# One ScalarE column write ahead of the load of the second x tile

## The chip, the cores and the metric

The kernel runs on one core of one Trainium2 chip. The metric is the device time of one execution in microseconds, as the median of several runs. A profile of one further execution gives the start and duration of every instruction, the DMA packets, and what each engine waited for.

A core has five engines that run side by side, each with its own instruction stream: TensorE (PE in the profile, its weight loads PEld), VectorE (DVE), ScalarE (ACT), GpSimd (POOL) and SyncE (SP). Transfers are issued from the streams of SP, ACT and POOL; a transfer's issue stands in the order of that stream. They are carried by 16 DMA engines that all queues share.

## The reference

One layer of a streaming encoder on an input x of 512 positions by 1024 channels, in float32:

```
xn = RMSNorm(x)
[gate_a | gate_b | gMLP u, v | ssm z | ssm x, B, C | ssm dt] = xn @ W_in
y_a = gMLP spatial gating of u, v
y_b = Mamba-2 mixer (causal conv, chunked scan, SiLU gate, grouped RMSNorm)
m   = sigmoid(gate_a) * (y_a @ P_a) + sigmoid(gate_b) * (y_b @ P_b)
h   = x + m @ W_o
h   = h + ConvGLU-FFN(RMSNorm(h))
out = RMSNorm(h)
```

All that the change touches is how the first product of `xn @ W_in` gets its operands: the transposed input x and the first block of W_in.

## The kernel before

Channels lie on the 128 partitions and the 512 positions along the free dimension. x comes transposed, as eight tiles `xT[0]` to `xT[7]` of 128 channels by 512 positions, 256 KB each. `xT[0]` is part of a slightly larger tile `x0m`, which also carries the weights of the first norm as eight extra columns.

Every float32 operand of a product is split in two halves, `hi` (a rounded copy, made by ScalarE) and `lo` (the rest, made by VectorE). A product takes three matmuls: hi by hi, hi by lo, lo by hi (lines 101, 102 and 104 in `cols`). A block of weights reaches SBUF as `raw`; ScalarE makes `hi` from it and VectorE `lo`.

The first product is called B0 (256 output columns in two PSUM tiles). It runs on x times its norm weight without the division by the norm, which is applied later. It is ordered by k (`BYK`): for each x tile k six matmuls, so that it can begin when `xT[0]` and the first quarter of its weights are there. Its weights come as four transfers of 256 KB (tiles `first0` and `first4`, two k to a transfer). In this text f0a is the transfer for k = 0 and 1, f0b that for k = 2 and 3, f4a and f4b those after them.

The transfers of the start go out in this order from three streams (lines 158 to 171):

```
SP:    x0m, f0a, xT2, xT3, f4a, xT5, f4b, xT7, then the weights C0, wdt, constants, ...
ACT:   xT1, f0b
POOL:  xT4, xT6
```

Then ScalarE and VectorE prepare the operands in a fixed order (lines 189 to 202): `xw0` hi and lo, the weights of f0a hi and lo, `xw1`, `xw2`, the weights of f0b, `xw3`, `xw4`, the weights of f4a, and so on.

Ahead of all that stands a short prologue. GpSimd and VectorE fill constants, among them `one`, a column of ones. PE runs ten warm-up matmuls on a tile of ones (`WARM`, line 143; 20 in the profile, since each takes two passes), whose result nobody reads. ScalarE squares the column `one` in place (line 145); that makes it load its function table at the very start.

The order of this whole first stage is written out by hand for all five streams (`tc.manual_schedule`). After it only PE's order stays written out. The order of the other four streams is set by a planner that walks through a simulated time line of the whole program with its own costs for every instruction and transfer. The planner also allots buffers and places the semaphore waits, in the first stage too: an instruction that overwrites what another wrote waits for it.

Behind B0 come C0 (the same on the next weights), the sums of squares for the norm (`xss`), a small product `dtp`, the broadcast of the norm (`rbp`), and then some 30 products on the normed x, the scan, the gMLP, the merge and the FFN. At the very end one half of the last output tile is written by ScalarE (line 741) and its transfer out is issued from ScalarE's own stream (line 744).

Of the kernel before, what the change touches and what calls it, by code (L numbers as in the profile page):

```python
# [10 lines left out]
AF = mybir.ActivationFunctionType  # L11
# [22 lines left out]
def kernel(  # L34
# [6 lines left out]
    dve, act, pe, pool, sync = nc.vector, nc.scalar, nc.tensor, nc.gpsimd, nc.sync  # L41
# [8 lines left out]
    def T(name, dt=F32):  # L50
        return tp.tile([P, S], dt, tag="t", name=name)
# [4 lines left out]
    def PA(name):  # L56
        return pp.tile([P, S], F32, tag="aux", name=name, bufs=4)
# [4 lines left out]
    def f(t):  # L62
        return t.bitcast(F32)
# [72 lines left out]
    with tc.manual_schedule(engines={E.PE, E.Activation, E.DVE, E.SP, E.Pool}):  # L136
        ones = const.tile([P, P], F32, name="ones")
        pool.memset(ones, 1.0)  # L138
        one = const.tile([P, 1], F32, name="one")
        dve.memset(one, 1.0)  # L140
        warm = PA("warm")
        for i in range(WARM):
            pe.matmul(warm[:, 0:P], lhsT=ones, rhs=ones, start=True, stop=True)  # L143

        act.activation(out=one, in_=one, func=AF.Square)
        ident = const.tile([P, P], F32, name="ident")
        make_identity(nc, ident)
        mhalf = const.tile([P, 16], F32, name="mhalf")
        pool.memset(mhalf, -0.5)
        tri = const.tile([P, P], F32, name="tri")  # L150
        pool.memset(tri, 1.0)
        pool.affine_select(out=tri, in_=tri, pattern=[[1, P]], compare_op=ALU.is_ge, fill=0.0,
                           base=0, channel_multiplier=-1)


        x0 = const.tile([P, S + KD], F32, name="x0m")
        raws = []
        for k in range(KD):
            if k % 4 == 0:
                raw = wp.tile([P, 4, 2 * P], F32, tag="wraw", name=f"first{k}", bufs=4)  # L160
                raws.append(raw)
            if k == 0:
                sync.dma_start(out=x0, in_=x0_in)
                t = x0[:, 0:S]
            else:
                t = T(f"xT{k}")
                {1: act, 4: pool, 6: pool}.get(k, sync).dma_start(out=t, in_=xt_in[:, k, :])
            xT.append(t)
            if k % 2 == 0:
                q = slice(k % 4, k % 4 + 2)  # L170
                (act if k == 2 else sync).dma_start(out=raw[:, q, :], in_=w_in[U_B, k // 4][:, q, :])

        wdt = const.tile([P, KD, HEADS], F32, name="wdt")
        pcol = const.tile([P, R_ALL], F32, name="pcol")
        dtb = const.tile([P, HEADS], F32, name="dtb")
        alog = const.tile([P, HEADS], F32, name="alog")
        ahead_w = []
        for src, name in ((w_in[U_C, 0], "C0w0"), (w_in[U_C, 1], "C0w1")):
            raw = wp.tile([P, 4, 2 * P], F32, tag="wraw", name=name + "r", bufs=4)
            sync.dma_start(out=raw, in_=src)  # L180
            ahead_w.append(raw)
            if name == "C0w0":
                sync.dma_start(out=wdt, in_=wdt_in)
        sync.dma_start(out=pcol, in_=cols_in)
        sync.dma_start(out=dtb, in_=dtb_in[0].partition_broadcast(P))
        sync.dma_start(out=alog, in_=alog_in[0].partition_broadcast(P))


        for k in range(KD):
            h = T(f"xw{k}h", F32R)  # L190
            m = x0[:, S + k:S + k + 1]
            act.activation(out=h, in_=xT[k], func=AF.Copy, scale=m)
            l = T(f"xw{k}l", F32R)
            dve.scalar_tensor_tensor(out=l, in0=xT[k], scalar=m, in1=f(h), op0=ALU.mult, op1=ALU.subtract)
            xw.append((h, l))
            if k % 4 == 0:
                ahead.append([wp.tile([P, 4, 2 * P], F32R, tag=f"w{n}", name=f"B0w{k}{n}") for n in ("hi", "lo")])
            if k % 2 == 0:
                hi, lo = ahead[-1]
                raw, q = raws[k // 4], slice(k % 4, k % 4 + 2)  # L200
                act.activation(out=hi[:, q], in_=raw[:, q], func=AF.Copy)
                dve.tensor_tensor(out=lo[:, q], in0=raw[:, q], in1=f(hi)[:, q], op=ALU.subtract)
# [396 lines left out]
    for i in range(0, 16, 2):  # L599
        ssm_step()  # L600
        ps = cols(w_in, U_Z + i // 2, xn, f"z{i}")
        for q in range(2):
            t = i + q
# [14 lines left out]
    for i in range(0, 8, 2):  # L618
        ps = cols(wpa_in, i // 2, ya, f"pa{i}")
        for q in range(2):  # L620
            t = T(f"m{i + q}")
# [28 lines left out]
    for i in range(0, 8, 2):  # L650
        ps = cols(wo_in, i // 2, ms, f"wo{i}")
        for q in range(2):
            k = i + q
# [172 lines left out]
```

## Time and profile before

| | |
|---|---|
| time, median of 3 runs | 1027.45 us (1027.16 to 1027.64) |
| time of the profiled execution | 1028.71 us |
| its span, first to last instruction | 1027.0 us |
| PE busy | 1014.9 us (99% of the span) |
| VectorE busy | 616.5 us |
| ScalarE busy | 450.2 us |
| first matmul of B0 begins | 6.36 us |
| mean DMA rate over the span | 107 GB/s |
| DMA rate in the first fortieth of the span | 273 GB/s |

The profiled execution takes 1.71 us more than its span, for what lies around the first and last instruction. All times below with two decimals are counted from the start of the span. In a timeline row the first number is the start, the second the duration, both in us; a bracket at the end gives how long the engine had been idle and what ended that. A stream's name with a q (ACTq, SPq) marks an issue of a transfer, not its carrying out. In rows of transfers the last number is the time from issue to landing.

### The profile page before, as it was taken

The page shows a single profiled execution, that of the slowest core. Times are in us where ns is not written, and L with a number is a line of the kernel's source. Part 1 is how long each engine was busy: PE and PEld are TensorE (multiplying, and loading weights), DVE is VectorE, ACT ScalarE, POOL GpSimd, SP SyncE. Part 2 cuts the span into 40 slices and gives each one's busy share as a digit, 9 for nine tenths or more (in the row PEclk, how much of TensorE's full clock was granted, in tenths as well). Part 3 has the DMA queues.
Part 4 walks back from the last instruction along what each step waited for, and adds up shares of the span by engine and source line. Part 5 has one row for each costly group of instructions (what it writes and reads, how often), then busy time and mean ns, then how long its engine had stood idle before and what let it go on. Part 6 is the DMA issues. An engine that isn't in the chain of part 4 may idle for free.

```text
span 1027.0 us, 12488 instructions
## 1 busy us (share of the span) xinstructions
PE 1014.9 (99%) x4856; PEld 840.3 (82%) x4856; DVE 616.5 (60%) x1006; ACT 450.2 (44%) x613; POOL 41.9 (4%) x72
## 2 busy tenths in 40 slices
PE   9999899999999999999999999999999999999997
PEld 7888788888888888888888888888888888888885
DVE  7795987878796554354123445477668677742224
ACT  7465675665564333363322223354444444331122
POOL 1000000220000200000000000000000000000000
PEclk9999899999999999999999999999999999999999
DMA  7323445423333233323322332232223233323302
GB/s 273 110 83 111 151 144 165 143 94 121 114 125 113 72 97 110 113 85 100 102 97 88 103 102 86 100 114 92 91 93 96 91 101 103 97 89 103 99 25 83
DMA packets 36157, 109.85 MB, mean 107 GB/s; under 512 B 4657, under 2 KB 4929, under 8 KB 36097
## 3 DMA queue, kind: packets, MB, share of 16 engines
q1 hardware_dynamic: 35056, 106.68, 31.8%
q0 software_dynamic: 608, 1.58, 0.5%
q8 instruction: 38, 0.62, 0.3%
q10 hardware_dynamic: 432, 0.79, 0.2%
q14 instruction: 23, 0.18, 0.1%
HBM read 106.80 MB, written 2.24 MB: 106 GB/s over the span
## 4 chain that ended last, share of the span: by engine, by line
PE 98%; DMA 1%; issue 0%; DVE 0%; ACT 0%; POOLq 0%; POOL 0%; SPq 0%
PE dn L726 11%; PE vp L526 1%; PE vp L528 1%; PE vp L527 1%; PE pb6p L101 1%; PE pb4p L101 1%; PE pb2p L101 1%; PE pb0p L101 1%; PE pb6p L104 1%; PE pb4p L104 1%; PE pb2p L104 1%; PE pb0p L104 1%; PE pb6p L102 1%; PE pb4p L102 1%; PE pb2p L102 1%; PE pb0p L102 1%
## 5 line engine op out<-in xcount | busy, mean ns | idle before, releaser
L397 ACT ACT_TABLE_LOAD x15 | 19.2, 1283 | 3.1 <-DMA s15bc<-acum_d 1.6
L764 POOL TENSOR_TENSOR fsr<-fs,mhalf 128x1 f32<-128x1 f32 x4 | 2.2, 548 | 354.9 <-DVE fs L762 354.9
L657 ACT ACTIVATE hh<-hT,pcol 128x512 fp32r<-128x512 f32 x8 | 5.8, 722 | 15.0 <-DVE hT L655 15.0
L756 ACT ACTIVATE fj<-htok 128x512 f32<-128x512 f32 x8 | 5.1, 632 | 16.6 <-DVE htok L754 16.6
L345 ACT ACT_TABLE_LOAD x8 | 10.3, 1283 | 3.9 <-DVE B2c L343 3.0
L214 POOL TENSOR_TENSOR hrr<-hrv,mhalf 128x4 f32<-128x4 f32 x1 | 1.0, 1042 | 248.0 <-DVE hrv L212 248.0
L631 DVE TENSOR_TENSOR m<-m,sa 128x512 f32<-128x512 f32 x8 | 5.5, 688 | 8.6 <-ACT sa L630 8.6
L754 DVE TENSOR_TENSOR htok<-dn,htok 128x512 f32<-128x512 f32 x8 | 5.5, 692 | 8.0 <-PE dn L726 7.9
L612 DVE TENSOR_TENSOR yq<-yq,zs 128x512 f32<-128x512 f32 x12 | 8.2, 685 | 1.5 <-ACT zs L611 1.4
L562 PEld LDWEIGHTS sp<-wsT,v 128*128 128x128 f32 x64 | 7.8, 191 | 0.3
L659 DVE SCALAR_TENSOR_TENSOR hl<-hT,pcol,hh 128x512 fp32r<-128x512 f32 x8 | 6.0, 747 | 3.2 <-ACT hh L657 3.2
L562 PE MATMUL sp<-wsT,v 128*128 128x128 f32 x64 | 7.8, 275 | 0.0
L538 DVE BATCH_NORM_STATS2 bst<-v 128x6 f32<-128x128 f32 x32 | 7.1, 280 | 0.3
L534 ACT ACTIVATE v<-vp 128x512 f32<-128x512 f32 x8 | 4.8, 594 | 3.6 <-PE vp L528 3.6
L565 DVE SCALAR_TENSOR_TENSOR sv<-sp,pcol,radd 128x512 f32<-128x512 f32 x8 | 6.0, 746 | 0.0
L343 DVE SCALAR_TENSOR_TENSOR B2c<-B2p,pcol,B2c 128x511 f32<-128x511 f32 (+2 forms) x6 | 4.2, 742 | 2.5 <-ACT B2c L341 2.5
L694 ACT COPY htok<-htp 128x512 f32<-128x512 f32 x8 | 4.7, 588 | 2.3 <-PE htp L692 2.3
L143 PE MATMUL warm<-ones 128*128 128x128 f32 x20 | 4.6, 429 | 1.1 <-POOL ones L138 1.1
L568 DVE TENSOR_TENSOR sv<-sv,gu 128x512 f32<-128x512 f32 x8 | 5.5, 688 | 0.3
L645 DVE TENSOR_TENSOR sb<-sb,m 128x512 f32<-128x512 f32 x8 | 5.5, 689 | 0.1
L343 DVE SCALAR_TENSOR_TENSOR x14c<-x14p,pcol,x14c 128x511 f32<-128x511 f32 (+2 forms) x6 | 4.5, 747 | 1.5 <-ACT x14c L341 1.4
L743 DVE SCALAR_TENSOR_TENSOR htok<-htok,fsr,fnw 128x512 f32<-128x512 f32 x7 | 5.0, 745 | 0.7 <-POOL fsr L764 0.7
(4034 smaller groups left out, 3501.2 us busy)
## 6 DMA issues: line engine op xcount, KB each, us to landing
out_dram<-htok SPq DMA_DIRECT2D x7, 256.0 KB, 2.0
xT<-in_xt_dram SPq DMA_DIRECT2D x4, 256.0 KB, 6.8
yrb<-yr_d POOLq DMA_DIRECT2D x4, 256.0 KB, 3.5
first<-in_w_in_dram SPq DMA_DIRECT2D x3, 256.0 KB, 7.0
xT<-in_xt_dram POOLq DMA_DIRECT2D x2, 256.0 KB, 7.0
C0w0r<-in_w_in_dram SPq DMA_DIRECT2D x1, 512.0 KB, 7.4
C0w1r<-in_w_in_dram SPq DMA_DIRECT2D x1, 512.0 KB, 7.3
x0w0r<-in_w_in_dram SPq DMA_DIRECT2D x1, 512.0 KB, 5.3
```

The source lines that it names most:

```text
L101: pe.matmul(ps[i], lhsT=hi[:, k, c], rhs=xh, start=(kb == 0 and k == 0), stop=False)
L102: pe.matmul(ps[i], lhsT=hi[:, k, c], rhs=xl, start=False, stop=False)
L104: pe.matmul(ps[i], lhsT=lo[:, k, c], rhs=xh, start=False, stop=(kb == nb - 1 and k == 3))
L343: dve.scalar_tensor_tensor(out=c[:, j:], in0=u[:, :S - j], scalar=pc(R_CW + 24 * (3 - j) + t), in1=c[:, j:], op0=ALU.mult, op1=ALU.add)
L345: act.activation(out=c, in_=c, func=AF.Silu)
L397: act.activation(out=bc, in_=bc, func=AF.Exp)
L526: pe.matmul(ps[t], lhsT=xh[:, ts], rhs=hi[:, k, :], start=(kb == 0 and k == 0), stop=False)
L527: pe.matmul(ps[t], lhsT=xl[:, ts], rhs=hi[:, k, :], start=False, stop=False)
L528: pe.matmul(ps[t], lhsT=xh[:, ts], rhs=lo[:, k, :], start=False, stop=(kb == 3 and k == 1))
L562: pe.matmul(sp[:, t * P:(t + 1) * P], lhsT=vn[t][b][:, gg:gg + P], rhs=wsT[b][:, gg:gg + P], start=True, stop=True)
L612: dve.tensor_tensor(out=acc, in0=acc, in1=zs, op=ALU.add)
L726: pe.matmul(po[t][b], lhsT=l[:, ts], rhs=r[:, cs], start=(k == 0 and l is xh and r is hi), stop=(k == NFF - 1 and r is lo))
```

## The change

For k = 1 ScalarE writes the first column of the new tile `xT1` (the square of the column `one`, so ones) just ahead of the issue of that tile's load from ScalarE's own stream. The load then overwrites the column together with the rest of the tile, so what is computed stays the same. Since the load overwrites what ScalarE wrote, its issue has to come after that write.

```
                 t = T(f"xT{k}")
+                if k == 1:
+                    act.activation(out=t[:, 0:1], in_=one, func=AF.Square)
                 {1: act, 4: pool, 6: pool}.get(k, sync).dma_start(out=t, in_=xt_in[:, k, :])
```

No instruction is removed and no transfer is added.

## The prediction

> **What bounds the kernel now.** I read the page first, then the chain of waits, then the timeline of the first 23 us.
>
> ```profile
> span 1027.0 us, 12488 instructions
> PE 1014.9 (99%) x4856; PEld 840.3 (82%) x4856; DVE 616.5 (60%) x1006; ACT 450.2 (44%) x613; POOL 41.9 (4%) x72
> PE 98%; DMA 1%; issue 0%; DVE 0%; ACT 0%; POOLq 0%; POOL 0%; SPq 0%
> ```
>
> PE sets the time. It is idle for about 12 us in all, so the change can help only by starting PE's gapless run earlier, or by moving one of its few gaps. The start, as the timeline has it:
>
> ```profile
> 0.80 1.28 ACT L145 ACT_TABLE_LOAD   x1 [0.80 <-PEq L817]
> 0.80 0.38 SPq L163 DMA_DIRECT2D x0m<-in_x_dram  x1
> 0.97 0.38 ACTq L167 DMA_DIRECT2D xT<-in_xt_dram  x1
> 1.06 4.64 PE L143 MATMUL warm<-ones 128*128 128x128 f32 x20 [1.06 <-POOL ones L138]
> 1.39 0.45 ACTq L171 DMA_DIRECT2D first<-in_w_in_dram  x1
> 2.09 0.20 ACT L145 ACTIVATE one<-one 128x1 f32<-128x1 f32 x1
> 4.06 0.72 ACT L192 ACTIVATE xw0h<-x0m 128x512 fp32r<-128x512 f32 x1 [1.77 <-DMA x0m<-in_x_dram]
> 5.68 0.63 ACT L201 ACTIVATE B0w0hi<-first 128x512 fp32r<-128x512 f32 x1 [0.89 <-DMA first<-in_w_in_dram]
> 6.36 0.50 PE L101 MATMUL B0p<-xw0h,B0w0hi 128*128 128x512 f32 x1 [0.66 <-ACT B0w0hi L201]
> 7.37 0.72 ACT L192 ACTIVATE xw2h<-xT,x0m 128x512 fp32r<-128x512 f32 x1 [0.45 <-DMA xT<-in_xt_dram]
> 8.83 0.73 ACT L192 ACTIVATE xw3h<-xT,x0m 128x512 fp32r<-128x512 f32 x1 [0.21 <-DMA xT<-in_xt_dram]
> 9.59 0.75 DVE L194 SCALAR_TENSOR_TENSOR xw3l<-xT,x0m,xw3h 128x512 fp32r<-128x512 f32 x1
> 10.79 0.39 PE L102 MATMUL B0p<-xw3l,B0w0hi 128*128 128x512 f32 x1
> ```
>
> ScalarE's stream issues its two transfers (xT1 and f0b) at 0.97 and 1.39, while the table load of 0.80 to 2.08 is still running: an issue does not wait for it. PE finishes its warm-up at 5.70 (1.06 + 4.64), then sits for 0.66 us until the weights of f0a are there. The landings, from the rows of transfers (the second xT row is xT2, issued at 1.71; the third xT3, issued at 2.18) and the chain of waits (the last row):
>
> ```profile
> x0m<-in_x_dram SPq DMA_DIRECT2D x1, 260.0 KB, 3.2
> xT<-in_xt_dram ACTq DMA_DIRECT2D x1, 256.0 KB, 3.8
> first<-in_w_in_dram ACTq DMA_DIRECT2D x1, 256.0 KB, 4.9
> xT<-in_xt_dram SPq DMA_DIRECT2D x1, 256.0 KB, 5.6
> xT<-in_xt_dram SPq DMA_DIRECT2D x1, 256.0 KB, 6.6
> 1.24 4.41 DMA first<-in_w_in_dram
> ```
>
> Issue plus time to landing gives the order x0m 4.0, xT1 4.77, f0a 5.65, f0b 6.29, xT2 7.31, xT3 8.78. So xT1, issued from ScalarE's stream, passes between x0m and f0a, though PE needs f0a first. The queues' shares of 3 to 4 us show this (q10 is ScalarE's queue, q1 SyncE's):
>
> ```profile
> q10 hardware_dynamic: 99, 0.18, 70.6%
> q1 hardware_dynamic: 28, 0.04, 10.5%
> ```
>
> **The change part by part.** *The added instruction* is of the form of the 2.09 row, 0.20 us. ScalarE is idle from 2.29 to 4.06 (1.77 us, the bracket of xw0h), so it costs nothing; without that cover it would cost 0.20. It needs no other table.
>
> *The wait.* For an issue that waits for ScalarE's own write, the end of the kernel has a pattern:
>
> ```profile
> 1022.43 0.72 ACT L741 ACTIVATE htok<-htok,fsr 128x512 f32<-128x512 f32 x1 [0.85 <-POOL fsr L764]
> 1023.18 0.38 ACTq L744 DMA_DIRECT2D out_dram<-htok  x1
> ```
>
> The write ends at 1023.15, the issue comes 0.03 later. Here the write runs from 2.29 to 2.49, so xT1 is issued at 2.52 instead of 0.97, and f0b, queued behind it, at about 2.94 (the spacing of 0.42 stays) instead of 1.39; the second issue is over at 3.39. Next in ScalarE's stream is xw0h at 4.06, so 0.67 us of slack remain. SP's and POOL's streams hold nothing that waits for this.
>
> The Trainium skill, ScalarE: Activation LUTs, section What ACT_TABLE_LOAD costs, speaks against this: it adds a drain of about 1380 ns to the 1283 ns of a load. The trace has the 1283 (first row above) but the ACTIVATE 0.01 us behind it, so no drain shows. By the page both issues would come 1.38 later, the second over at 4.77, and f0b would drift towards rival B; the sum would then be a loss of B's size.
>
> *The order of the transfers.* The shortest time to landing in the rows is 3.2 (x0m, nothing ahead of it). So xT1 lands at 5.72 at the earliest and f0b at 6.14; f0a, issued at 1.24, could land from 4.44 on and now has only x0m ahead of it. It takes xT1's place and lands near 4.77 instead of 5.65. The bounds are 4.77 and 5.65; I take 4.77, since the shares show one queue's transfer going through nearly whole before the other's next. Then xT1 and xT2 share the places at 5.65 and 6.29, and f0b has the one at 7.31. xT3 has the same bytes ahead of it in either order, so it stays at 8.78. With xT1 between 5.72 and 6.29 its halves take ScalarE and VectorE until 7.24 to 7.80 (0.72, 0.75 and a wait of 0.04 between them); the second matmul of k = 1, which needs them, stood at 8.07 (12 matmuls of 0.227 ahead of the 10.79 row), so that a gain of 0.27 to 0.8 is allowed here. I take the early end, as nothing else is due at that place but xT2, of which PE has need later.
>
> *What PE gets from it.* xw0h still runs 4.06 to 4.78, the weights' hi then 4.80 to 5.43, and PE could begin at 5.48, but its warm-up holds it until 5.70: 0.66 us earlier. Part of this is run at half clock. The granted clock and PE's busy time in some stretches:
>
> ```profile
> 105.00:106.00 1.00, 0.00 (x0) 0.00 (x0) 1.00 (x4) 0.00 (x0) 0.00 (x0) 0.64 0.94 289
> 106.00:112.00 6.00, 5.93 (x14) 4.70 (x15) 6.00 (x16) 5.91 (x7) 0.00 (x0) 0.50 0.94 283
> 112.00:113.00 1.00, 1.00 (x5) 0.80 (x5) 1.00 (x5) 1.00 (x1) 0.00 (x0) 0.95 0.61 150
> 1023.00:1024.00 1.00, 0.00 (x0) 0.00 (x0) 0.18 (x1) 0.15 (x1) 0.00 (x0) 0.73 0.00 0
> 2.88:6.29 3.41, 2.81 (x14) 2.52 (x12) 0.75 (x1) 1.34 (x3) 0.44 (x1) 1.00 0.93 305
> 105.28:108.69 3.41, 2.62 (x6) 2.15 (x7) 3.41 (x9) 2.66 (x3) 0.00 (x0) 0.50 1.00 240
> ...
> L562 PE MATMUL sp<-wsT,v 128*128 128x128 f32 x64 | 7.8, 275 | 0.0
> ...
> 106.83 0.43 PE x8p L102
> 112.54 0.23 PE x8p L102
> ```
>
> The column ahead of the DMA share is the clock: half from 105.28 (0.64 is 0.72 us at 0.5) to 112.10, half again from 1023.46. The gaps, 6.82 and from the first to the last 918.18, are 2 and 269 steps of 3.41 us, and 29 steps back from 105.28 lies 6.29. The view lists no half clock at the start, but the warm-up passes take 0.23 us each (4.64 / 20) where the same form at L562 takes 0.12 (7.8 / 64), so I put the first full clock at 6.29. From 5.70 to 6.29 PE does 0.59 x 0.23 / 0.43 = 0.32 us of work and loses 0.27. The gain is 0.66 - 0.27 = 0.39.
>
> *What is late next.* xT3: xw3l is ready at 10.34, so the matmul at 10.79 can come 0.40 earlier at most (0.05 for the wait, as from 6.31 to 6.36 in the first rows). This just allows 0.39. Further on, the sums of squares:
>
> ```profile
> 21.39 0.69 DVE L240 TENSOR_TENSOR xq<-xq,xq 128x512 f32<-128x512 f32 x1
> 22.81 0.95 PE L222 MATMUL xss<-ones,xq 128*128 128x2 f32 x8
> ```
>
> They are ready at 22.08 against 22.81, so 0.3 remain. Behind them everything hangs on the norm, which PE broadcasts, and moves along.
>
> **The sum:** 0 for the write, -0.39 at the start. The profiled execution would go from 1028.71 to 1028.32; it is 1.26 above the median of the runs (1027.45), so for the runs **1027.1 us** (1027.06). Bounds: no gain at all to 0.66; its own range is 1026.7 to 1027.5. The 0.2% that a measurement of this kernel can tell from no change is 2.05 us, five times the gain.
>
> **The rivals.** The one real gap in the middle prices three of them:
>
> ```profile
> 106.07 0.76 PE L101 MATMUL x8p<-xn0h,x8w0h 128*128 128x512 f32 x1 [3.47 <-DVE B2c L343]
> 104.59 0.68 DVE L395 TENSOR_SCALAR s0bc<-s0bc,ac_k 128x128 f32<-128x128 f32 x3 [1.11 <-DMA s0bc<-acum_d]
> 105.19 0.74 DVE L343 SCALAR_TENSOR_TENSOR B2c<-B2p,pcol,B2c 128x509 f32<-128x509 f32 x1
> ```
>
> *A, the clock at the gap.* PE stops at 102.60 (106.07 - 3.47) and the clock halves at 105.28. If the 3.41 us steps stand still against the kernel's start, PE comes back 0.39 earlier into the same half clock and gives back 0.39 x (1 - 0.23 / 0.43) = 0.18: 1027.25. But the step of 105.28 to 108.69, busy for 2.62 and not enough to restore the clock, would then be busy for 3.01, more than the 2.81 after which the first full clock came. Full clock at 108.69 would save 3.41 x 0.47 = 1.59 more: 1025.6. For it: the 2.62 and the 2.81. Against it: nothing shows that busy time decides. The Trainium skill, TensorE: Matmul & The Clock Gate, Part 1, has a window of 3413 ns, which the steps match, that runs free of the kernel's start; by that the phase differs between executions, and the median keeps the 0.39.
>
> *B, f0b too late: slower.* ScalarE takes f0b's weights ahead of xw3h, in order. If f0b, issued 1.55 later, misses its turn and lands with xT3 at 8.8, hi runs 8.82 to 9.45, and PE's k = 2 loads its first weights at 9.50. Before, it did so at 8.98: its first matmul stood 7 matmuls ahead of the 10.79 row, at 9.20, and the load one step of 0.23 ahead of that. So 0.5 is lost: 1028.0. If it lands 1.1 later still (the landings of the first six stand 0.6 to 1.5 apart), it is 1.6 and 1029.1. It decides from a landing at 8.30 on (8.98 - 0.05 - 0.63). Against it: 6.14 is its earliest landing, two places ahead of that.
>
> *C, the planner.* From the norm on the orders of VectorE, ScalarE and SP come from a simulated time line, in which xT1 is now later. At the gap above VectorE waits 1.11 us for a transfer ahead of the last step of B2c. Turned around there, the gap and its half clock go: 3.47 + 6.03 x 0.47 = 6.3, 1021.1. A second such place costs as much: 1033.7. For it: ties are decided anew by any shift. Against it: a shift common to all streams changes no order, and the first stage's order is fixed.
>
> *D, the change does nothing:* the issue isn't held, or f0a lands no earlier: 1027.45. The pattern at L744 is against it.
>
> **How the numbers follow.** The forecast 0.52 (with the 1027.25 of A); A's early clock 0.08; B 0.12; C faster 0.08, slower 0.12; D 0.08. From 1025.3 to 1029.5 it holds all but C: 0.80. Faster by over 0.2%: C's 0.08 and 0.02 of A, 0.10. Slower by over 0.2%: C's 0.12 and 0.02 of B, 0.14. Within: 0.76.
>
> **What would show it.** Right: the ACTq issues at 2.5 and 2.9; f0a landing near 4.8; first B0 matmul at 5.5 to 5.7; xw3h still at 8.8; the x8p gap still 3.5. Wrong: f0a near 5.6; an idle PE ahead of k = 1 to 3; VectorE's order around B2c changed; or half clock ended at another step.

## The result: slower by 0.56%, and the profile after

The change makes the kernel slower. It took 1033.31 us (median of 6 runs, 1032.0 to 1034.29) against 1027.55 us for the kernel before in the same comparison (6 runs, 1025.9 to 1028.52): a ratio of 1.0056, with a 95% interval of 1.0045 to 1.0067. The forecast was 1027.1 us, with a range of its own of 1026.7 to 1027.5; its widest range, with the rivals but the planner's, went to 1029.5. The profiled execution took 1032.0 us, the shortest of the six; its span is 1030.3.

One sentence of the kernel's description above is too wide: PE's order stays written out by hand only for B0 and C0 (the `with` block from line 484 on in the listing of before), not behind them. On all five engines the order of instructions is the same with and without the change, apart from the one added ScalarE instruction.

The start of the changed kernel, as its timeline has it (start, duration, engine and line, in us; a bracket gives the idle time ahead and what ended it):

```profile
2.33 0.20 ACT L168 ACTIVATE xT<-one 128x1 f32<-128x1 f32 x1
2.56 0.41 ACTq L169 DMA_DIRECT2D xT<-in_xt_dram  x1
3.01 0.45 ACTq L173 DMA_DIRECT2D first<-in_w_in_dram  x1
3.62 0.72 ACT L194 ACTIVATE xw0h<-x0m 128x512 fp32r<-128x512 f32 x1 [1.09 <-DMA x0m<-in_x_dram]
4.25 0.61 ACT L203 ACTIVATE B0w0hi<-first 128x512 fp32r<-128x512 f32 x1
5.35 0.54 PE L101 MATMUL B0p<-xw0h,B0w0hi 128*128 128x512 f32 x1
6.42 0.63 PE L104 MATMUL B0p<-xw0h,B0w0lo 128*128 128x512 f32 x2
9.51 0.72 ACT L194 ACTIVATE xw1h<-xT,x0m 128x512 fp32r<-128x512 f32 x1 [4.65 <-DMA xT<-in_xt_dram]
10.28 0.50 PE L101 MATMUL B0p<-xw1h,B0w0hi 128*128 128x512 f32 x1 [3.23 <-ACT xw1h L194]
11.07 0.50 PE L102 MATMUL B0p<-xw1l,B0w0hi 128*128 128x512 f32 x1 [0.28 <-DVE xw1l L196]
22.11 0.39 PE L101 MATMUL C0p<-xw0h,C0w0h 128*128 128x512 f32 x1
```

The write and the two held issues are where they were expected. x0m comes earlier too (xw0h begins at 3.62 instead of 4.06), f0a's weights are there at 4.25, and B0 begins at 5.35, 1.01 earlier than before. Then PE does the six matmuls of k = 0 and waits 3.23 us, because xT1 lands only at 9.5. C0, which follows B0 without a gap, begins at 22.11. In the kernel before it began here:

```profile
17.37 0.39 PE L101 MATMUL C0p<-xw0h,C0w0h 128*128 128x512 f32 x1
```

So 4.74 us are lost by the end of B0. PE's waits in the changed kernel (in all, times, longest) name the new one, of the size of the old one at x8p:

```profile
PE B0p L101 <- ACT xw1h L194: 3.2, 1, 3.2
PE x8p L101 <- DVE B2c L345: 3.2, 1, 3.2
PE B0p L102 <- DVE xw1l L196: 0.3, 1, 0.3
```

In the chain of work that ended last, the transfer of xT1 now stands as its longest transfer (start, length):

```profile
2.56 6.92 DMA xT<-in_xt_dram
```

The landings of the changed kernel, in rows of transfers (the last number is the time from issue to landing), in the order of their issues: f0a (1.24), xT2 (1.71), xT4 (2.03), xT3 (2.18), xT1 (2.56), f4a (2.65), f0b (3.01):

```profile
first<-in_w_in_dram SPq DMA_DIRECT2D x1, 256.0 KB, 3.0
xT<-in_xt_dram SPq DMA_DIRECT2D x1, 256.0 KB, 6.5
xT<-in_xt_dram POOLq DMA_DIRECT2D x1, 256.0 KB, 6.2
xT<-in_xt_dram SPq DMA_DIRECT2D x1, 256.0 KB, 7.7
xT<-in_xt_dram ACTq DMA_DIRECT2D x1, 256.0 KB, 6.9
first<-in_w_in_dram SPq DMA_DIRECT2D x1, 256.0 KB, 8.0
first<-in_w_in_dram ACTq DMA_DIRECT2D x1, 256.0 KB, 7.8
```

Added to the issues they give 4.2, 8.2, 8.2, 9.9, 9.5, 10.7 and 10.8. Three things differ from before. First, xT1 is the sixth transfer to be issued instead of the second (x0m is ahead of the list), and it lands fifth, behind xT2 and xT4. Second, the transfers behind f0a all land late and close together; xT2, issued at 1.71 as before, takes 6.5 us instead of 5.6. The windows show what the DMA engines did meanwhile (length, busy time and instructions of PE, PEld, DVE, ACT and POOL, then PE's clock, the busy share of the DMA engines and GB/s). Before:

```profile
4.00:6.00 2.00, 1.70 (x8) 1.40 (x7) 0.75 (x1) 1.05 (x2) 0.00 (x0) 1.00 0.98 338
6.00:8.00 2.00, 1.64 (x7) 1.38 (x8) 1.37 (x2) 1.55 (x4) 0.00 (x0) 1.00 1.04 408
```

After:

```profile
4.00:6.00 2.00, 2.00 (x11) 1.92 (x11) 1.35 (x2) 0.86 (x2) 0.00 (x0) 1.00 0.70 211
6.00:8.00 2.00, 1.04 (x5) 0.52 (x3) 0.00 (x0) 0.00 (x0) 0.00 (x0) 1.00 0.94 361
...
12.30:15.72 3.42, 3.42 (x9) 2.64 (x8) 3.42 (x6) 3.42 (x7) 0.00 (x0) 0.50 0.92 318
111.29:114.70 3.41, 3.41 (x9) 2.65 (x9) 3.41 (x9) 3.35 (x5) 0.00 (x0) 0.50 0.98 239
```

From 4 to 6 us the DMA engines moved 211 GB/s where they moved 338 before, with their share at 0.70 instead of 0.98, although eleven transfers had been issued by 4 us (x0m had landed by then, f0a followed at 4.2). This lower rate by itself does not make xT1 late. Over the first 8 us the mean rate was 223 GB/s against 247, which is less by 0.19 MB, under one transfer. And a kernel of the experiments below (both streams held) moved 219 GB/s from 4 to 6 us and 273 from 6 to 8, with xT1 issued at the same 2.56, and had it landed at 7.2.

What differs there is how much of the engines' time xT1's queue got (the rows stand below, with that kernel). From 6 to 8 us in the changed kernel three queues are carried side by side (q0 is GpSimd's, q10 ScalarE's, q1 SyncE's):

```profile
q0 software_dynamic: 87, 0.30, 37.6%
q10 hardware_dynamic: 125, 0.24, 32.3%
q1 hardware_dynamic: 95, 0.18, 23.8%
```

This is how the Trainium skill, DMA: Bandwidth & Descriptors, section Queues, rings and completion order, describes it: each engine goes round between the queues that have work. By it, xT1 gets a third of the engines here, not a place of its own; the trace agrees, with 32.3%. From 5 to 6 us, though, ScalarE's queue had only 3.8%, some 3 us after xT1's issue, and the record does not show why.

The third difference is the clock, in the last two windows of the fence headed After: the 3.23 us gap is followed by one step of 3.42 us at half clock (matmuls 0.43 apart instead of 0.23), which the kernel before did not have there, and the gap at x8p is followed by one such step instead of two.

**The account of the profiled execution**, from B0's begin to C0's: 16.76 us (22.11 - 5.35) against 11.01 (17.37 - 6.36), 5.75 more. The waits are 3.51 of it (3.23 + 0.28), the half clock 1.59 (3.42 x (1 - 0.23 / 0.43)), and the remaining 0.65 goes with matmuls that stand further apart than 0.23 beside the gaps (10.28 to 11.07 is 0.79, of which only 0.28 is listed as a wait). Less the earlier begin of 1.01, the loss is 4.74. At x8p one step of half clock less gives back some 1.6, which is why this one execution is only 3.3 us longer than the profiled one of before, while the medians are 5.8 apart. The other five executions of the changed kernel took 1033.1 to 1034.3 us at a mean granted clock of 0.993, where the profiled one had 0.995: 0.2% of the span, about one more step of half clock, by estimate.

### The profile page after: what moved, and what is told of

The parts are those of the page before. It is cut to its first block, busy times and chain, and to the rows that moved or that the text cites. A ratio compares the mean times of both kernels' runs of the same rounds, so it can differ in the third digit from the quotient of the medians.

```text
span 1030.3 us, 12489 instructions
## 1 busy us (share of the span) xinstructions
PE 1015.6 (99%) x4856; PEld 840.4 (82%) x4856; DVE 616.2 (60%) x1006; ACT 450.1 (44%) x614; POOL 41.9 (4%) x72
## 4 chain that ended last, share of the span: by engine, by line
PE 97%; DMA 1%; issue 0%; ACT 0%; DVE 0%; POOLq 0%; POOL 0%
PE dn L728 11%; PE vp L528 1%; PE vp L530 1%; PE vp L529 1%; PE pb6p L104 1%; PE pb4p L104 1%; PE pb2p L104 1%; PE pb0p L104 1%; PE pb6p L102 1%; PE pb4p L102 1%; PE pb2p L102 1%; PE pb0p L102 1%; PE pb6p L101 1%; PE pb4p L101 1%; PE pb2p L101 1%; PE pb0p L101 1%
```

## The experiments

The kernel before measured between 1027.4 and 1027.9 us (medians) in these comparisons; each ratio is to the runs of before beside it. All diffs are against the changed kernel unless it is said otherwise, and show the changed lines alone; "..." marks lines left out.

### What holds the issues: the tile, or the instruction's own wait?

One kernel lets ScalarE square `one` into a spare column, so that nothing overwrites xT1 and its load need not follow:

```
+        spare = const.tile([P, 1], F32, name="spare")
-                    act.activation(out=t[:, 0:1], in_=one, func=AF.Square)
+                    act.activation(out=spare, in_=one, func=AF.Square)
```

> ScalarE writes the same square into a spare column that nothing loads, so neither transfer of its stream is held. Theory (all of the loss is the late issue of xT1): xT1 is issued at 0.97 and lands near 4.8, the first B0 matmul stands at 6.36, no gap ahead of k = 1; time within 0.2% of before, 1027.5. Rival (the added instruction itself, or another state of the program, costs): 1029 or more.

It measured 1031.74 us, a ratio of 1.0036 [1.0024, 1.0047]: slower than before, with no tile to wait for. Its timeline:

```profile
2.33 0.20 ACT L169 ACTIVATE spare<-one 128x1 f32<-128x1 f32 x1
2.33 0.38 ACTq L170 DMA_DIRECT2D xT<-in_xt_dram  x1
2.75 0.45 ACTq L174 DMA_DIRECT2D first<-in_w_in_dram  x1
```

The issues still came late, only 0.23 to 0.26 earlier than with the change. The second kernel has the same instruction with another input, the tile `ones`, which GpSimd has written by 1.0 (against the kernel just shown):

```
-                    act.activation(out=spare, in_=one, func=AF.Square)
+                    act.activation(out=spare, in_=ones[:, 0:1], func=AF.Square)
```

> As in the spare column run, but the added square reads the tile of ones that POOL wrote instead of the column that ScalarE itself squared just before, so it doesn't wait for ScalarE. Theory (in the spare column run the issues stood behind the added instruction's own wait for ScalarE, and the instruction itself is free): the ACTq issues are at 1.0 to 1.5 again, xT1 lands at 4.8 to 5.9, no gap over 0.5 ahead of k = 1, 1027.2 to 1028.2. Rival (a second instruction behind the table load holds the stream, whatever it waits for): issues at 2.0 or later and 1031 or more.

It measured 1027.46 us, 0.9991 [0.9981, 1.0002]:

```profile
1.04 0.37 ACTq L170 DMA_DIRECT2D xT<-in_xt_dram  x1
1.45 0.45 ACTq L174 DMA_DIRECT2D first<-in_w_in_dram  x1
2.09 0.20 ACT L145 ACTIVATE one<-one 128x1 f32<-128x1 f32 x1
2.20 0.19 ACT L169 ACTIVATE spare<-ones 128x1 f32<-128x1 f32 x1
```

Here the issues stand behind the same number of ScalarE instructions and go out at 1.04 and 1.45, ahead of both. So an issue passes instructions that are only queued or running, the table load among them. What it does not pass is an instruction that itself waits for a result: the added square reads `one`, which ScalarE writes until 2.29. The instruction is free (0.9991); its wait holds the queue, and the overwritten column adds about 0.25 us to that.

### Which late transfer costs: xT1 or f0b?

The column is written in f0b's tile instead, so that only f0b is held:

```
-                if k == 1:
-                    act.activation(out=t[:, 0:1], in_=one, func=AF.Square)
...
+                if k == 2:
+                    act.activation(out=raw[:, 2, 0:1], in_=one, func=AF.Square)
```

> The column is written into the tile of f0b, so xT1 goes out at 0.97 as before and only f0b is held, to about 2.5. Theory (transfers of all queues are carried in the order of their issue): x0m, xT1, f0a, xT2, xT4 and xT3 go ahead of f0b, which lands at 8.8 to 10.5 instead of 6.29; f0a stays at 5.65 or comes slightly earlier, PE loses 0.5 to 2 us ahead of k = 2: 1028 to 1030. Rival (queues take turns, one transfer each): f0b lands at 7.3 at the latest and the time is that of before, 1027.5.

It measured 1028.05 us, 1.0001 [0.9992, 1.0011]. f0b went out at 2.56 and landed at 9.9 (7.3 us), PE waited 1.16 us for it ahead of k = 2, and no clock step followed at the start. C0 began at 18.90, 1.53 later than before, yet the runs don't tell it from before. (Where C0 begins in a single profile is a rough guide: the kernel with the filled x8 gap below has the start of before, and C0 began there at 19.60, since its first full clock came at 10.70 instead of 6.29.) So rival B's mechanism exists, but it is small. In the changed kernel PE waits for xT1 and has no listed wait for f0b, so the loss goes with xT1; no run holds xT1 alone.

### A shorter hold, and no second queue at all

A GpSimd memset of the same column, in place of ScalarE's square, lets xT1 go at 1.59 and f0b at 2.04:

```
+        x1 = T("xT1")
+        pool.memset(x1[:, 0:1], 0.0)
...
-                t = T(f"xT{k}")
-                if k == 1:
-                    act.activation(out=t[:, 0:1], in_=one, func=AF.Square)
+                t = x1 if k == 1 else T(f"xT{k}")
```

> The column of xT1 is written by POOL (a memset that ends near 1.6) instead of ScalarE, so ScalarE's stream issues xT1 at about 1.6 and f0b at about 2.0: behind f0a (1.24), but xT1 ahead of xT2 (1.71) and f0b ahead of xT3 (2.18). Theory (order of issue): landings in the order x0m, f0a, xT1, xT2, f0b, xT3; f0a near 4.2 to 4.8, xT1 near 5.2 to 5.9; B0 begins at 5.35 to 5.7 with no gap over 0.5 us; the time falls by 0.3 to 1.0 us, 1026.5 to 1027.2. Rival (SP's queue goes first, ScalarE's gets through only when SP has none waiting): xT1 lands behind xT3 at 8 or later, a gap of 2 or more ahead of k = 1, 1030 or more.

It measured 1027.88 us, 0.9998 [0.9988, 1.0008]. xT1 landed at 6.46, and PE's timeline shows what the earlier begin is worth:

```profile
5.42 0.50 PE L101 MATMUL B0p<-xw0h,B0w0hi 128*128 128x512 f32 x1 [0.39 <-ACT B0w0hi L203]
7.26 0.51 PE L101 MATMUL B0p<-xw1h,B0w0hi 128*128 128x512 f32 x1 [0.18 <-ACT xw1h L194]
8.10 0.50 PE L102 MATMUL B0p<-xw1l,B0w0hi 128*128 128x512 f32 x1 [0.34 <-DVE xw1l L196]
```

B0 begins 0.94 earlier, but C0 begins at 17.81, 0.44 later than before: B0 runs at the pace at which its tiles arrive, and an early begin turns into gaps. The next kernel is the one before the change, with xT1 and f0b issued from SyncE's stream in the order of need (the diff is against the kernel before):

```
-                {1: act, 4: pool, 6: pool}.get(k, sync).dma_start(out=t, in_=xt_in[:, k, :])
+                {4: pool, 6: pool}.get(k, sync).dma_start(out=t, in_=xt_in[:, k, :])
-                (act if k == 2 else sync).dma_start(out=raw[:, q, :], in_=w_in[U_B, k // 4][:, q, :])
+                sync.dma_start(out=raw[:, q, :], in_=w_in[U_B, k // 4][:, q, :])
```

> The kernel before with xT1 and f0b issued from SP too, in the order x0m, f0a, xT1, xT2, f0b, xT3, f4a, ...; ScalarE's stream issues none, and its table load holds nothing. Theory (what counts is the order in which the tiles come, and the rate of the transfers caps it): f0a lands at 4.2 to 4.8 and B0 begins at 5.3 to 5.7, but the gaps ahead of k = 1 to 3 add up to 0.5 to 1.2, since the tiles of k = 1 to 3 come at the pace of the transfers; time within 0.1% of before. Rival (an early f0a is worth what it brings B0's start): 1026.6 or less.

It measured 1028.83 us, 1.0013 [1.0002, 1.0024]. f0a landed at 4.53 and xT1 at 5.73, but f0b, issued at 2.66, at 9.59, with a gap of 1.29 us ahead of k = 2. One stream alone issues about 0.47 us apart, and so f0b is issued behind GpSimd's xT4 (2.03).

### How much of the loss is half clock?

In the changed kernel 13 matmuls that nobody reads (26 passes) are put between k = 0 and k = 1, into PE's gap:

```
-            for o in order:
+            for n, o in enumerate(order):
+                if name == "B0" and kb == 0 and n == 4:
+                    for _ in range(FILL):
+                        pe.matmul(warm[:, 0:P], lhsT=ones, rhs=ones, start=True, stop=True)
```

> The changed kernel with 13 more matmuls on the tile of ones (26 passes of about 0.12 us, 3.2 us in all, result unread) in PE's order between k = 0 and k = 1 of B0, where PE now stands idle for 3.2 us. The transfers and the x tiles come as late as before; only PE's idleness is taken away. Theory (the wait costs its 3 us and then a step of half clock): the half clock of 12.3 to 15.7 is gone and the time falls by 1.0 to 2.0 us, to 1031.3 to 1032.3. Rival (the clock there isn't due to the idle PE, or the filler ends late): 1033.3 or more.

It measured 1031.37 us, 1.0032 [1.0019, 1.0044], 1.9 us less than the change by the medians and about 2.5 by the two ratios to before. Its timeline:

```profile
6.89 3.07 PE L115 MATMUL warm<-ones 128*128 128x128 f32 x26
10.60 0.49 PE L101 MATMUL B0p<-xw1h,B0w0hi 128*128 128x512 f32 x1 [0.64 <-ACT xw1h L197]
```

The clock stayed full, and the k = 1 matmuls came no earlier. So some 2 us are what the idle PE costs beyond the wait itself; the 0.32% that remain are the late tile (C0 begins at 20.82, 3.45 later than in the kernel before).

The changed kernel was also profiled once more:

> The changed kernel once more, for another execution's profile. If xT1's lateness belongs to the order of the issues, it lands between 9 and 10 again and PE waits about 3 us ahead of k = 1; if it was an accident of one execution, it lands near 6. If the clock moves in 3.41 us steps whose phase differs between executions, the half clock behind the same gap starts at another distance from it, or is missing, or lasts two steps.

It took 1032.93 us. xT1 landed at 10.31 and PE waited 3.93 us, so the late tile is no accident of one execution. The half clock there lasted two steps (9.11 to 15.93). Over the profiles of all kernels, gaps of 2.8 to 3.9 us were followed by none, one or two steps of 3.41 us: at the start, none behind 2.79 and 3.05, one behind 3.23, two behind 3.12 and 3.93. The length of the gap does not decide it alone.

### Why xT1 lands at 9.5

The theory at this point: transfers land nearly in the order of their issues over all queues, so xT1 pays for what is now issued ahead of it. The rival: a second queue that begins late is slow by itself. First GpSimd's two loads were given to SyncE. In this kernel and the next the planner orders much behind B0 anew, so only the start is compared:

```
-                {1: act, 4: pool, 6: pool}.get(k, sync).dma_start(out=t, in_=xt_in[:, k, :])
+                {1: act}.get(k, sync).dma_start(out=t, in_=xt_in[:, k, :])
```

> The changed kernel, with xT4 and xT6 issued from SP's stream instead of POOL's, in the order of k. SP then issues x0m, f0a, xT2, xT3, xT4, f4a, ...; ScalarE's xT1 still at about 2.56, between xT3 (2.18) and xT4 (2.65). Theory (order of issue): xT1 is carried right behind xT3 and lands at 6.3 to 7.5 instead of 9.46, and PE's gap ahead of k = 1 falls from 3.2 to under 1.3. Rival 1 (SP's queue goes first as long as it has work): xT1 lands at 9 or later, the gap stays 3 or more. Rival 2 (only POOL's transfers held xT1): the same early landing as the theory, so the place of xT1 behind or ahead of xT2 and xT3 tells: by rival 2 xT1 lands ahead of xT3. The planner's orders behind B0 change here, so the time is not compared, only the first 20 us.

It took 1029.82 us (one run): xT1 landed at 8.09, 5.5 us from its issue, and PE waited 2.22 us. Then they were left on GpSimd's queue, but held back behind ten memsets until 4.88:

```
+                if k == 4:
+                    for _ in range(10):
+                        pool.memset(t[:, 0:P], 0.0)
```

> The changed kernel with ten memsets of POOL ahead of its issue of xT4, so that POOL's two transfers begin about 2 us later; xT1 is issued at 2.56 as in the changed kernel. Some orders behind B0 change, so only the first 12 us are compared. Theory (the transfers of POOL's queue, which began at 4.4 in the changed kernel, keep xT1 back): ScalarE's queue moves its first packets at about 4.3 instead of 5.8 and xT1 lands at 6.5 to 7.5 instead of 9.5, with a gap under 1.3 ahead of k = 1. Rival (xT1 stands behind SP's xT2 and xT3 alone): 5.8 and 9.5 stay, the gap is 3.

It took 1033.78 us (one run). With GpSimd's loads out of the way xT1 still landed at 9.3, and PE waited 3.05 us:

```profile
xT<-in_xt_dram ACTq DMA_DIRECT2D x1, 256.0 KB, 6.8
```

Then SyncE's loads behind f0a were held, by giving xT2 a column write too, so that it went out at 3.22:

```
-                if k == 1:
+                if k in (1, 2):
```

> The change, and the same column write for xT2 too, so that SyncE's stream stops behind f0a until about 2.8 us and xT2, xT3, f4a and all that follows are issued behind xT1 (2.56) instead of up to 0.85 us ahead of it. If xT1 lands late because the transfers of SyncE issued ahead of it are carried with it, xT1 lands at 5.5 to 6.5, PE's gap ahead of k = 1 is under 1 us and there is no half clock at the start; the later tiles come late instead, and the time is 1027.5 to 1030. If ScalarE's queue is slow whenever it begins late, or the other queues get the DMA engines first in any case, xT1 lands at 9 or later, the gap stays near 3.2 us and the time is 1033 or more.

This measured 1032.21 us, 1.0042 [1.0028, 1.0056]. xT1 landed at 9.6 and the gap was 3.12 us:

```profile
xT<-in_xt_dram ACTq DMA_DIRECT2D x1, 256.0 KB, 7.0
```

Each of the two alone speaks for the rival. Both at once do not (`if k in (1, 2, 4):`, so that nothing but x0m and f0a is issued ahead of xT1), once as a single execution and once timed:

> The change, and the column write for xT2 and xT4 too, so that SyncE's and GpSimd's transfers behind f0a all go out after xT1 (2.56). xT1 is then third by the order of the issues, with only x0m and f0a ahead of it. If what is issued ahead makes it late, SyncE's or GpSimd's, it lands at 5.2 to 6.2, and PE waits under 1 us ahead of k = 1. If a second queue that begins late is slow for itself, xT1 lands at 8 or later although nothing is ahead of it, and the gap is 2 us or more.

> The change with SyncE's and GpSimd's transfers behind f0a held until xT1 is issued, timed. In one profile xT1 landed at 7.52 and C0 began at 18.61, 1.24 later than in the kernel before and 3.50 earlier than with the change alone. If the loss of the change is the wait for xT1 and its half clock, the time is 1028 to 1029.5, some 4 to 5 us under the change. If the change costs elsewhere too, or the held transfers cost behind C0 what they gain ahead of it, it is over 1031.

xT1's transfer in the single execution:

```profile
xT<-in_xt_dram ACTq DMA_DIRECT2D x1, 256.0 KB, 5.0
```

And in the profile of the timed one:

```profile
xT<-in_xt_dram ACTq DMA_DIRECT2D x1, 256.0 KB, 4.6
```

With both held xT1 landed at 7.5 and 7.2 instead of 9.5, PE waited 1.05 and 0.62 us ahead of k = 1, and the timed one took 1028.41 us, 1.0002 [0.9993, 1.0011] (the single execution 1026.67). The change's loss is gone, although ScalarE's two issues are as late as in the change. So the loss comes from the transfers that are issued ahead of xT1 or close behind it, and those of either stream alone are enough to cause it. The share of ScalarE's queue from 5 to 6 us shows the difference, in the changed kernel and then in the timed one:

```profile
q10 hardware_dynamic: 6, 0.01, 3.8%
q10 hardware_dynamic: 158, 0.29, 94.9%
```

This share is not the whole account: with one stream held it was 54 and 58% in that microsecond, and xT1 landed no earlier than in the change. What the queue had carried when xT1 landed says more. xT1 and f0b have 0.26 MB each, and both go over ScalarE's queue. The rows count from 0 to xT1's landing, in the kernel before (to 4.77), the changed one (to 9.48) and the timed one (to 7.15):

```profile
q10 hardware_dynamic: 144, 0.26, 19.6%
q10 hardware_dynamic: 246, 0.46, 13.1%
q10 hardware_dynamic: 276, 0.50, 29.2%
```

Before the change xT1 was carried first and f0b after it. Behind the hold most of f0b was carried before the last piece of xT1 (0.49 and 0.50 MB with one stream held too), so that xT1 landed only when nearly all that its queue had was through. Why the pieces of xT1 come so unevenly there stays open.

The theory of the order is too simple, all the same: with only x0m and f0a ahead xT1 should have landed near 6, and it needed 4.6 to 5.0 us where the kernel before took 3.8 with x0m ahead of it. In the kernel with SyncE's held, the DMA engines moved only 212 GB/s from 4 to 6 us and 262 from 6 to 8. What lowers their rate there stays open, but it is as low in the timed kernel with both held (219 and 273), where xT1 landed at 7.2. With SyncE's held the trace shows packets that take up to 1.3 us beside the usual 0.08, but not what they wait for.

### Versions that try to keep the gain

If the order of the issues decides, f0a gets second place by trading queues with xT1, without any hold (against the kernel before):

```
-                {1: act, 4: pool, 6: pool}.get(k, sync).dma_start(out=t, in_=xt_in[:, k, :])
+                {4: pool, 6: pool}.get(k, sync).dma_start(out=t, in_=xt_in[:, k, :])
-                (act if k == 2 else sync).dma_start(out=raw[:, q, :], in_=w_in[U_B, k // 4][:, q, :])
+                (act if k in (0, 2) else sync).dma_start(out=raw[:, q, :], in_=w_in[U_B, k // 4][:, q, :])
```

> The kernel before without the write, with two transfers exchanged: f0a goes out from ScalarE's stream (0.97) and xT1 from SyncE's (1.24). All issue times stay. If transfers land in the order of their issues whatever queue they are on, f0a takes the second place (4.8), xT1 the third (5.6), f0b, xT2 and xT3 keep 6.3, 7.3 and 8.8; B0 begins at 5.5 to 5.7 instead of 6.36, PE waits nowhere long ahead of k = 1 to 3, and C0 begins at 16.9 to 17.3; the time is 1026.9 to 1027.4, better than both kernels by a little. If the second queue's transfer only comes second because it is x's, or if the earlier start just turns into gaps as in the kernel with the write on GpSimd, C0 stays at 17.4 or later and the time at 1027.6.

It measured 1026.77 us, 0.9993 [0.9984, 1.0002]. f0a landed at 4.54, xT1 at 6.01, f0b at 6.71, xT2 at 7.35, xT3 at 9.00: the order of the issues, though each is now on the other queue. PE had no gap in B0:

```profile
0.97 0.86 ACTq L171 DMA_DIRECT2D first<-in_w_in_dram  x2
4.56 0.63 ACT L201 ACTIVATE B0w0hi<-first 128x512 fp32r<-128x512 f32 x1
5.34 0.75 PE L101 MATMUL B0p<-xw0h,B0w0hi 128*128 128x512 f32 x1
```

C0 began at 17.29, only 0.08 earlier than before for an early begin of 1.02, part of which ran at half clock (until 5.94). By itself this can't be told from no change.

The other version fills the gap at x8p, where the profile of before shows two steps of half clock (against the kernel before, behind the `ssm_step` ahead of x8):

```
+        if i == 8:
+            fill = PA("fill")
+            for _ in range(14):
+                pe.matmul(fill[:, 0:P], lhsT=ones, rhs=ones, start=True, stop=True)
```

> The kernel before, without the change, and 14 idle matmuls (28 passes of 0.12 us) of a constant tile into a PSUM tile of their own, behind the transposes of s0xt and ahead of x8p, where PE otherwise waits 3.47 us for B2c. If a gap of that length costs, beside itself, one or two steps of 3.41 us at half clock (1.6 us each), and filling it keeps the clock, the time falls by 1.6 to 3.2 us, to 1024.5 to 1026, with no half clock between 100 and 120 us. If the clock is halved by something else, or the planner's new order behind it costs as much, it stays at 1027.5 or rises.

It measured 1027.45 us, 0.9991 [0.9982, 1.0001], less than expected. In its profile the clock at x8p stayed full, but the first full clock of the kernel came only at 10.70 and C0 at 19.60. Both together:

> The kernel before with f0a and xT1 exchanged between the two queues and the 14 idle matmuls ahead of x8p, without the column write. Each alone measured 0.9993 [0.9984, 1.0002] and 0.9991 [0.9982, 1.0001]. If both are real, small and independent (an earlier start, a clock that stays full), the ratio is near 0.9984, 1025.8, with its interval under 1. If they were scatter, it is 1.000.

1025.41 us, a ratio of 0.9974 [0.9963, 0.9984]: faster than both kernels. Its rows at x8p (timeline):

```profile
102.17 3.29 PE L516 MATMUL fill<-ones 128*128 128x128 f32 x28
106.21 0.47 PE L101 MATMUL x8p<-xn0h,x8w0h 128*128 128x512 f32 x1 [0.75 <-DVE B2c L343]
```

The wait for B2c is filled but for 0.75 us, x8p begins where it did, and the window from 102 to 112 has the clock at 1.00:

```profile
102.00:112.00 10.00, 9.25 (x58) 8.07 (x56) 8.48 (x22) 6.49 (x9) 0.00 (x0) 1.00 0.88 279
```

The pair gives 2.5 us where the two alone gave 0.7 and 0.1 by their medians (1.6 by their ratios). The intervals of the two alone reach down to 0.9984 and 0.9982. The single times fit two sources of scatter, one of which each kernel alone leaves: with the filled gap nine of ten runs have a granted clock of 0.999 (which leaves out the time ahead of the first full clock), but lie in two groups, 1025.6 to 1025.9 and 1027.3 to 1028.1; with the traded queues the time goes with the clock, from 0.999 at 1025.4 to 0.995 at 1028.4; and the eight runs of the pair all lie between 1025.1 and 1026.06. That the two need each other was not tested. With the fill the planner also orders some instructions behind x8 anew, on PE, VectorE and ScalarE (from 120 us on in the profiles); PE has no listed wait there in either kernel, and no run separates this from the clock.

## Why the prediction was wrong, step by step

- **The added instruction** was right: 0.20 us at 2.33, ScalarE idle around it, 0.9991 for the instruction without its wait.
- **The wait** was right in its times (2.56 and 3.01 against 2.52 and 2.94), and only half right in its reason: the hold comes from the square's own wait for `one` (issues at 2.33 and 2.75 with a spare column), not mainly from the overwritten tile. No drain of 1.38 us behind the table load showed in any run here.
- **The order of the transfers** failed, and everything followed from it. f0a's part was right (4.2 to 4.25 against 4.77). But xT1 was given "5.72 at the earliest" and then the places at 5.65 and 6.29 beside xT2. It landed at 9.5, because it now had to share the engines with xT2, xT4 and xT3, issued ahead of it. The shares of 3 to 4 us were read as one queue's transfer going nearly whole before the other's; from 6 to 8 us three queues moved side by side (37.6, 32.3 and 23.8%). With both other streams held, xT1 landed at 7.2 to 7.5 and the loss was gone (1.0002); even then it took 4.6 to 5.0 us, so 5.72 was out of reach. The rows of before held a warning already: the issues there, 0.80, 0.97, 1.24, 1.39, 1.71, 2.18, land in just that order on whatever queue, at 4.0, 4.77, 5.65, 6.29, 7.31, 8.78. An issue at 2.56 stands behind the last of them, so by them 8.8 or later was to be expected, and for f0b more (a guide only: with SyncE's loads held xT1 landed at 9.6 with fewer ahead). xT3, taken to stay at 8.78, landed at 9.9. The lower bound (issue plus the shortest time to landing) was used as if it were the value.
- **What PE gets** was too low at the start (1.01 instead of 0.66: xw0h, taken to stay at 4.06, began at 3.62, and the matmul began at 5.35 although the rows put the warm-up's end near 5.65), and without any weight against what followed.
- **What is late next** named xT3, with 0.40 of room. It was xT1, with a wait of 3.23 us that was followed by half clock; the prediction asked about half clock only at the start and at x8p. Filling this gap gave back some 2 us. An idle PE ahead of k = 1 to 3 stood in the prediction's own list of what would show it wrong.
- **Rival B** had the right kind of mechanism (a held transfer loses its place and PE waits in B0) but looked only at f0b, at 0.5 to 1.6 us and a chance of 0.12. Held alone, f0b costs nothing that can be told (1.0001); the wait that the changed kernel shows is for xT1.
- **Rival A**: the clock steps do stand free against the kernel's start. The last half clock at the start ends at 15.72 and the next begins at 111.29, 28 steps of 3.413 us apart, but the first full clock came at 5.48 here, 6.29 before, 5.69 in the change's other profile. The Trainium skill, TensorE: Matmul & The Clock Gate, Part 1, says the window is free-running, and the trace agrees. This scatter is 1.6 us a step, more than the gain that was forecast.
- **Rival C** did not happen: no engine's order changed. **Rival D** did not either: the issues were held and f0a landed earlier.

## What to carry to other kernels

Before a transfer's issue is moved, list all issues of all queues by time and read their landings beside them: before and after the change and with the traded queues the transfers landed nearly in the order of their issues, and a hold of 1.6 us put xT1 behind four others and cost 4.7 us in landing. The order is a guide and no law: with one stream held xT1 had fewer ahead of it and was as late. Issue plus the shortest landing seen is a bound and no estimate, and a wait that it opens on TensorE is to be priced with the half clock that may follow it. And an instruction put ahead of an issue is free only if it has nothing to wait for itself.

## What the runs showed of the hardware

- An issue from ScalarE's stream passed a running table load and queued instructions (issued at 0.97 and 1.04, during the load of 0.80 to 2.08), but not an instruction that waits for ScalarE's own earlier result (2.33).
- The same transfers issued in another order moved more slowly for a while: 211 GB/s instead of 338 from 4 to 6 us, at a busy share of 0.70 while transfers were outstanding (223 instead of 247 over the first 8 us). The landing of xT1 did not go with this rate: at 219 GB/s it landed at 7.2 instead of 9.5.
- Holding back either of two streams did not help a transfer (6.8 and 7.0 us to landing against 6.9), holding back both did (4.6 to 5.0). When a held xT1 (0.26 MB) landed, its queue had carried 0.46 to 0.50 MB, most of f0b with it; unheld, 0.26.
- PE gaps of about 3 us were followed by none, one or two steps of 3.41 us at half clock, and their length alone did not decide it; 13 or 14 idle matmuls in such a gap kept the clock full.
